# Six column tiles at once behind a norm, and weight splits placed by due time, in a two-layer decoder trunk

## The chip, the cores and the metric

One core of one Trainium2 chip runs the kernel. The metric is the device time of one execution in microseconds (us), lower is better; the number given is the median of three runs.

## What is computed

A two-layer decoder trunk on a sequence of 256 tokens, width 2048, in float32. Each layer projects x with w_in into the inputs of two parallel head groups (a gated linear recurrence and a sparse attention with compressed, selected and sliding branches), joins them with w_out, normalizes, runs a gated FFN with a causal convolution of width 3, and normalizes again:

```python
for l in range(DEPTH):                      # DEPTH = 2
    h = x @ w_in[l]                         # 2048 -> 6704 columns
    hq, hf, hi, hg, nq_, kc, vc, ks_, vs_, kw, vw, gt = jnp.split(h, offsets, axis=-1)
    o_h = hgrn2_mixer(hq, hf, hi, hg, lower_bounds[l], hgrn_norm_w[l])
    o_n = nsa_mixer(nq_, kc, vc, ks_, vs_, kw, vw, gt, pos, cmp_pe_k[l], cmp_pe_v[l],
                    cmp_w1_k[l], cmp_w2_k[l], cmp_w1_v[l], cmp_w2_v[l])
    y = jnp.concatenate([o_h, o_n], axis=-1) @ w_out[l]
    x = layer_norm(DN_ALPHA * x + y, ln1_g[l], ln1_b[l])
    f = conv_ffn(x, w_up[l], conv_w[l], conv_b[l], w_down[l])   # 2048 -> 2 x 5632 -> 2048
    x = layer_norm(DN_ALPHA * x + f, ln2_g[l], ln2_b[l])
```

## The kernel before, in words

**Numbers in two parts.** Every float32 operand is held as a high part (rounded to the format that TensorE takes in one pass) and a low part. `split` (L231 to L236) makes them from a raw tile: the high part `whi` with a copy on ScalarE (L235), or on GpSimd (L233) for some units, the low part `wlo` with a subtraction on VectorE (L236). x lies in SBUF with the features on the partitions, as `self.x[:, k, part, token]`, k = 0 to 15 being the contraction tile. One weight block of 128 x 128 costs two matmuls: L317 multiplies the high part with both parts of x (512 columns), L318 the low part with x's high part (256 columns).

**Units.** Weights come in units of 8 blocks, 512 KB, one DMA each, in the order in which they are used. `blocks` writes that order down as (column tile c, contraction tile k): mostly all 16 k of a column tile, then the next tile. Behind a norm, where x comes one k at a time, the first `OUTER = 4` column tiles are done together, k outermost, and then one tile after the other. `run` walks through all units of both layers: it issues loads 7 units ahead, splits 3 units ahead and then emits the unit's matmuls. There are 5 raw buffers and 4 pairs of split ones. A split is emitted at high priority; after a norm, `self.barriers` holds instructions of the norm behind which the next splits have to stand on VectorE. The order within each engine is set by a list scheduler that plans with these priorities; on the chip each engine runs its list in order.

**PSUM.** Accumulators are banks: three `pj`, two `ps_s`, two `ps_t`, one `ps_h`. Column tiles take `pj`; the fourth of the tiles done together takes `ps_h` (`wide`). When a tile's last k is done, `total` evicts it: a copy on ScalarE (L356), an addition on VectorE (L357).

**The norm** (`norm`) works feature tile by feature tile: `less` subtracts the mean for four at a time (L895), L950 scales, ScalarE makes the high part (L954; for k=0 VectorE does, L952), L957 the low part. Statistics come from matmuls with a matrix of ones; a few matmuls of constants (L865) stand in the wait. `dg` (L912, L917) spreads the scale over the partitions.

**The projection's order** is `u` in `layer`: column pairs 0 to 2 (compressed, selected and sliding keys, tiles 0 to 5, twelve units), then eight value-and-gate units (w_vg, 560 wide, L345 to L347), between which stand four units of the compressed branch (w_c1, L1113, not split, so that each keeps its raw buffer until it is used), then pair 3, the same again, and the rest. L1113 multiplies `F0`, which `cmp_in` (L429) makes on VectorE from column pair 0 after the rotation (L382, L384, L385); L414 makes the low part of a rotated key. GpSimd splits from the projection's unit 20 on.

**The start** (`head`) loads and splits the first four units in pieces, x's first quarter first.

Of the kernel before, what the change touches and what calls it, by code (L numbers as in the profile page):

```python
# [29 lines left out]
F32 = mybir.dt.float32  # L30
# [9 lines left out]
S = 256  # L40
D = 2048
KT = D // 128
DFF = 5632
FT = DFF // 128
# [21 lines left out]
VG = 280  # L66


def blocks(cts, nk, outer=0, head=0):

    first, rest = cts[:outer], cts[outer:]
    if head:
        o = [(c, k) for c in first for k in range(head)]
        o += [(c, k) for c in first for k in range(head, nk)]
    else:
        o = [(c, k) for k in range(nk) for c in first]
    return o + [(c, k) for c in rest for k in range(nk)]


N_IN = 40
OUTER = 4
ORDER_IN = blocks(range(6), KT, outer=OUTER) + blocks(range(6, N_IN), KT)
ORDER_OUT = blocks(range(KT), KT, outer=3, head=12)
ORDER_UP = blocks(range(2 * FT), KT, outer=OUTER)
ORDER_DOWN = blocks(range(KT), FT)


# [4 lines left out]
URGENT = 4  # L94
POOL = 20

WARM = 9, 7

ROW = (slice(0, 64), slice(64, 128))
# [2 lines left out]
class Trunk:  # L102
# [144 lines left out]

    def head(self, units):

        pieces = [(0, 0, 256), (1, 0, 384), (0, 256, 512), (1, 384, 768), (0, 512, 1024),  # L250
                  (1, 768, 1024), (2, 0, 512), (3, 0, 512), (2, 512, 1024), (3, 512, 1024)]
        raws = [self.t(self.wp, [128, 1024], F32, "raw", bufs=RAW_BUFS) for _ in units]
        outs = {n: [self.t(self.wp, [128, 1024], F32R, tag, bufs=PART_BUFS) for tag in ("whi", "wlo")]
                for n in (1, 3)}
        for i, lo, hi in pieces:
            self.nc.sync.dma_start(raws[i][:, lo:hi], units[i][0][:, lo:hi])
        for i, lo, hi in pieces:
            q = slice(lo, hi)
            if i in outs:
                self.split(outs[i][0][:, q], outs[i][1][:, q], raws[i][:, q])  # L260
            else:
                k = slice(2 * i + lo // 256, 2 * i + hi // 256)
                self.split(self.x[:, k, 0], self.x[:, k, 1],
                           raws[i][:, q].rearrange("p (k t) -> p k t", t=256))
        for n in outs:
            units[n][3](*outs[n])
# [28 lines left out]
            self.load = loads.get(i + 1)  # L295
            units[i][3](*parts.pop(i))

    def units(self, src, order, act, nk, done, pump=1, pre=None, last=None, wide=None):


        st = {}
        mm = self.nc.tensor.matmul

        def cb(hi, lo, n):
            for i, (c, k) in enumerate(order[n:n + 8]):
                if pre is not None and (c, k) in pre:
                    pre[c, k]()
                if c not in st:
                    st[c] = (self.t(self.ps_h, [128, 2, S], F32, "h") if c == wide
                             else self.t(self.pj, [128, 2, S], F32, "pj"))  # L310
                x, out, o = act(k), st[c], slice(128 * i, 128 * i + 128)
                if c == last:
                    for p in range(2):
                        mm(out[:, 0], hi[:, o], x[:, p], start=k == 0 and p == 0, stop=False,  # L314
                           skip_group_check=True)
                else:
                    mm(out, hi[:, o], x, start=k == 0, stop=False, skip_group_check=True)  # L317
                mm(out[:, 0], lo[:, o], x[:, 0], start=False, stop=k == nk - 1,  # L318
                   skip_group_check=True)
                if k == nk - 1:  # L320
                    done(c, st.pop(c))
                if pump == 2 and i == 3:
                    self.pump(1)
            self.pump(1)

        return [(src(n // 8), 1024, True, lambda hi, lo, n=n: cb(hi, lo, n), LOOK_SPLIT)
                for n in range(0, len(order), 8)]
# [543 lines left out]
    def norm(self, l, which, last):  # L871

        nc, v, act = self.nc, self.nc.vector, self.nc.scalar.activation
# [65 lines left out]
        else:  # L939
# [20 lines left out]
                    los.append(queue(lo_of()))  # L960
            los.append(queue(lo_of()))

            self.barriers.extend(los[5::2])
        urgent.close()


# [53 lines left out]
    def layer(self, l):  # L1020
# [134 lines left out]
        for hp in range(4):  # L1155
            dones += [d_h(hp, slot) for slot in (0, 2, 3)]
        tiles = self.units(lambda n: a["w_in"][l, n], ORDER_IN, xin, KT,
                           lambda c, ps: dones[c // 2](c, ps), pump=2, pre={(0, 0): pre_in},
                           wide=OUTER - 1)

        def pairs(p, n=1):
            return tiles[4 * p:4 * (p + n)]
# [12 lines left out]
        for step in PLAN.split():  # L1175
# [7 lines left out]
            else:  # L1183
# [3 lines left out]
        u += self.units(lambda n: a["w_out"][l, n], ORDER_OUT, lambda k: self.o[k // 2][:, k % 2], KT, self.d_res(l, 0),  # L1187
                        pre={(0, 0): pre_att, (0, 8): pre_hgr, (0, 12): pre_out}, last=KT - 1)
        u += self.units(lambda n: a["w_up"][l, n], ORDER_UP, xin, KT, self.d_ff(l),
                        pre={(0, 0): pre_up}, wide=OUTER - 1)  # L1190
        u += self.units(lambda n: a["w_down"][l, n], ORDER_DOWN, lambda k: self.f[:, k], FT,
                        self.d_res(l, 1), pre={(0, 0): pre_down}, last=KT - 1)
        return u
# [1 line left out]
    def build(self):  # L1195
        self.setup()
        units = []
        for l in range(L):
            units += self.layer(l)

        xs = [(self.a["x"][kq], 1024, False, lambda raw, kq=kq: self.in_x(kq, raw), LOOK_SPLIT)
              for kq in range(4)]
        consts = (None, 0, False, lambda raw: self.load_consts(), LOOK_SPLIT)
        x0, x1, x2, x3 = xs
        self.run([x0] + units[:1] + [x1] + units[1:3] + [x2] + units[3:4] + [x3] + [consts]
                 + units[4:])
        self.finish()


# [113 lines left out]
```

## Time and profile before

| what | us |
|---|---|
| three timed runs | 2548.55, 2549.75, 2551.13 |
| median | 2549.75 |
| the profiled execution, its own time | 2539.28 |
| its span, first to last instruction | 2537.5 |
| PE busy in it | 2476.0 (98%) |
| VectorE (DVE) busy | 1782.0 (70%) |
| ScalarE (ACT) busy | 1197.6 (47%) |
| GpSimd (POOL) busy | 428.4 (17%) |
| DMA engines, mean rate | 172 GB/s |

The profile is one execution, and its times count from its first instruction. PE is the matmul unit, PEld its weight loads, DVE VectorE, ACT ScalarE, POOL GpSimd, SP the queue that issues the loads. Matmuls overlap each other, so that one row's duration is longer than the distance to the next one's start, and a busy PE is not a PE at its peak. A row's "idle before" is the time in which its engine did nothing, with the instruction that ended it.

### The profile page before, as it was taken

Reading aid. Unit: us, or ns where it says so; the run is one execution under the profiler, and the core shown is the slowest. Engines: PE = TensorE matmul, PEld = TensorE weight load, DVE = VectorE, ACT = ScalarE, POOL = GpSimd, SP = SyncE. Lnnn points to the kernel's source line nnn. Section 1 sums busy time; section 2 is a strip of 40 time slices with the busy share of each in tenths; the row PEclk is TensorE's granted clock in tenths of the full one; section 3 lists DMA queues with packets and bytes.
Section 4 is the critical chain, followed back from the end, with each engine's and each line's share of the span. In section 5 each row is a group of like instructions: output and inputs, shape, how many; then the busy total and the mean of one; then the engine's idle time right before and its main releaser. Section 6 shows DMA issues by size and latency. Waiting matters only on the chain. (4 is left out here: it accounts for less than half of the span.)

```text
span 2537.5 us, 41283 instructions
## 1 busy us (share of the span) xinstructions
PE 2476.0 (98%) x15993; PEld 2123.9 (84%) x15993; DVE 1782.0 (70%) x2705; ACT 1197.6 (47%) x2189; POOL 428.4 (17%) x403
## 2 busy tenths in 40 slices
PE   8999999999999999999989999999999999999997
PEld 7888878878888888888878888788788888888887
DVE  8767876787777777555597678767877777774554
ACT  4144425455555555334341444354655555553343
POOL 0444551300000000001014445413000000000111
PEclk9999999999999999999999999999999999999999
DMA  7644344545556565656546444445556566656563
GB/s 244 211 159 132 127 142 133 175 155 186 186 188 184 190 184 188 186 190 190 166 152 210 153 133 130 136 141 158 174 187 188 190 190 186 189 185 189 178 198 105
DMA packets 122884, 436.99 MB, mean 172 GB/s; under 512 B 13760, under 2 KB 14528, under 8 KB 122688
## 3 DMA queue, kind: packets, MB, share of 16 engines
q1 hardware_dynamic: 122688, 434.35, 53.6%
q8 instruction: 126, 2.06, 0.3%
q14 instruction: 70, 0.57, 0.1%
HBM read 432.20 MB, written 2.10 MB: 171 GB/s over the span
## 5 line engine op out<-in xcount | busy, mean ns | idle before, releaser
L317 PE MATMUL pj<-x,whi 128*128 128x512 f32 x4032 | 1435.1, 398 | 18.6 <-ACT whi L235 6.3
L236 DVE TENSOR_TENSOR wlo<-raw,whi 128x1024 fp32r<-128x1024 f32 (+2 forms) x819 | 1015.8, 1242 | 584.4 <-ACT whi L235 499.7
L318 PE MATMUL pj<-x,wlo 128*128 128x256 f32 x4032 | 1138.3, 283 | 4.0 <-DVE wlo L236 3.8
L235 ACT ACTIVATE whi<-raw 128x1024 fp32r<-128x1024 f32 (+2 forms) x631 | 661.7, 1049 | 827.7 <-PE pj L317 647.7
L317 PEld LDWEIGHTS pj<-x,whi 128*128 128x128 f32 x4032 | 758.9, 188 | 202.5 <-DVE x L957 12.5
L318 PEld LDWEIGHTS pj<-x,wlo 128*128 128x128 f32 x4032 | 757.0, 188 | 9.2 <-DVE wlo L236 6.1
L317 PE MATMUL pj<-f,whi 128*128 128x512 f32 x1320 | 460.4, 393 | 0.0
L318 PE MATMUL pj<-f,wlo 128*128 128x256 f32 x1408 | 395.3, 281 | 0.0
L317 PEld LDWEIGHTS pj<-f,whi 128*128 128x128 f32 x1320 | 247.2, 187 | 56.3
L233 POOL TENSOR_SCALAR whi<-raw 128x1024 fp32r<-128x1024 f32 (+1 forms) x188 | 215.3, 1148 | 331.6 <-PE pj L347 148.9
L318 PEld LDWEIGHTS pj<-f,wlo 128*128 128x128 f32 x1408 | 266.3, 189 | 0.1
L810 POOL TENSOR_TENSOR s<-z 128x512 f32<-128x512 f32 x4 | 8.2, 2059 | 1208.9 <-DVE z L807 1208.9
L982 DVE SCALAR_TENSOR_TENSOR ct<-ch,par,ct 128x255 f32<-128x255 f32 (+1 forms) x352 | 168.2, 481 | 6.0
L317 PE MATMUL pj<-o,whi 128*128 128x512 f32 x480 | 167.1, 392 | 2.0 <-DVE o L582 1.9
L318 PE MATMUL pj<-o,wlo 128*128 128x256 f32 x512 | 143.3, 281 | 0.0
L317 PEld LDWEIGHTS pj<-o,whi 128*128 128x128 f32 x480 | 89.7, 187 | 22.5 <-DVE o L582 2.4
L980 ACT ACTIVATE ct<-ch,par 128x256 f32<-128x256 f32 x176 | 102.9, 587 | 3.0 <-DVE ch L357 3.0
L318 PEld LDWEIGHTS pj<-o,wlo 128*128 128x128 f32 x512 | 96.8, 189 | 0.4
L347 PE MATMUL pj<-whi,x 128*128 128x280 f32 (+1 forms) x256 | 90.6, 355 | 0.0
L346 PE MATMUL pj<-wlo,x 128*128 128x280 f32 (+1 forms) x256 | 89.8, 352 | 0.0
L345 PE MATMUL pj<-whi,x 128*128 128x280 f32 (+1 forms) x256 | 89.3, 353 | 0.0
L357 DVE TENSOR_TENSOR ch<-pj,ch 128x256 f32<-128x256 f32 x174 | 72.4, 418 | 0.0
(240 smaller groups left out, 2141.3 us busy)
## 6 DMA issues: line engine op xcount, KB each, us to landing
raw<-w_up SPq DMA_DIRECT2D x352, 512.0 KB, 3.5
raw<-w_down SPq DMA_DIRECT2D x176, 512.0 KB, 3.6
raw<-w_in SPq DMA_DIRECT2D x158, 512.0 KB, 3.8
raw<-w_out SPq DMA_DIRECT2D x64, 512.0 KB, 3.6
raw<-w_v SPq DMA_DIRECT2D x32, 512.0 KB, 3.8
raw<-w_vg SPq DMA_DIRECT2D x32, 280.0 KB, 3.6
raw<-w_c SPq DMA_DIRECT2D x16, 512.0 KB, 3.7
out<-z SPq DMA_DIRECT2D x3, 512.0 KB, 2.6
```

Of the source, the lines that this page charges most:

```text
L233: self.nc.gpsimd.tensor_scalar(hi, raw, 1.0, 0.0, op0=ALU.mult, op1=ALU.add)
L235: self.nc.scalar.activation(hi, raw, AF.Copy)
L236: return self.nc.vector.tensor_sub(lo, raw, hi.bitcast(F32))
L317: mm(out, hi[:, o], x, start=k == 0, stop=False, skip_group_check=True)
L318: mm(out[:, 0], lo[:, o], x[:, 0], start=False, stop=k == nk - 1, skip_group_check=True)
L345: mm(st[tt], xh, wh, start=first, stop=False, skip_group_check=True)
L346: mm(st[tt], xh, wl, start=False, stop=False, skip_group_check=True)
L347: mm(st[tt], xl, wh, start=False, stop=kt == KT - 1, skip_group_check=True)
L357: self.nc.vector.tensor_add(out, ps[:, 0], out)
L810: add(self.s1, self.z[:, 0:2], zz)
L980: act(t[:, c], h[:, c], AF.Identity, scale=w[2], bias=w[3])
L982: v.scalar_tensor_tensor(t[:, c, s:], h[:, c, :S - s], w[n], t[:, c, s:], op0=ALU.mult, op1=ALU.add)
```

## The change

- `OUTER` is 6: behind each norm, and at the start, six column tiles are done together, for k = 0 to 13; `TAIL = 2`: the last two k's are done column by column. The same holds for w_in and w_up. The weights' layout in memory follows the new order.
- The fourth of the six tiles takes `ps_h`, the fifth and sixth take the two `ps_t` banks.
- The splits that follow a norm stand behind the low parts number 3, 5, 6, 8, 9, 10, 12, 13 and 14 (`AFTER`, nine splits); before, behind every second one from 5 on (six splits).
- At the start the first four units are x's first quarter, two weight units and x's second quarter, and the other quarters and the constants are spread out accordingly.

```diff
-def blocks(cts, nk, outer=0, head=0):
+def blocks(cts, nk, outer=0, head=0, tail=0):
...
-        o = [(c, k) for k in range(nk) for c in first]
+        o = [(c, k) for k in range(nk - tail) for c in first]
+        o += [(c, k) for c in first for k in range(nk - tail, nk)]
     return o + [(c, k) for c in rest for k in range(nk)]
...
-OUTER = 4
-ORDER_IN = blocks(range(6), KT, outer=OUTER) + blocks(range(6, N_IN), KT)
+OUTER, TAIL = 6, 2
+ORDER_IN = blocks(range(N_IN), KT, outer=OUTER, tail=TAIL)
 ORDER_OUT = blocks(range(KT), KT, outer=3, head=12)
-ORDER_UP = blocks(range(2 * FT), KT, outer=OUTER)
+ORDER_UP = blocks(range(2 * FT), KT, outer=OUTER, tail=TAIL)
...
+AFTER = 3, 5, 6, 8, 9, 10, 12, 13, 14
...
-        pieces = [(0, 0, 256), (1, 0, 384), (0, 256, 512), (1, 384, 768), (0, 512, 1024),
-                  (1, 768, 1024), (2, 0, 512), (3, 0, 512), (2, 512, 1024), (3, 512, 1024)]
+        pieces = [(0, 0, 256), (1, 0, 384), (1, 384, 768), (0, 256, 512), (1, 768, 1024), (2, 0, 512),
+                  (0, 512, 1024), (2, 512, 1024), (3, 0, 512), (3, 512, 1024)]
...
-                    st[c] = (self.t(self.ps_h, [128, 2, S], F32, "h") if c == wide
-                             else self.t(self.pj, [128, 2, S], F32, "pj"))
+                    if 3 <= c < wide:
+                        st[c] = (self.t(self.ps_h, [128, 2, S], F32, "h") if c == 3
+                                 else self.t(self.ps_t, [128, 2, S], F32, "t"))
+                    else:
+                        st[c] = self.t(self.pj, [128, 2, S], F32, "pj")
...
-            self.barriers.extend(los[5::2])
+            self.barriers.extend(los[k] for k in AFTER)
...
-        self.run([x0] + units[:1] + [x1] + units[1:3] + [x2] + units[3:4] + [x3] + [consts]
-                 + units[4:])
+        self.run([x0] + units[:2] + [x1] + units[2:6] + [x2] + units[6:8] + [x3] + [consts]
+                 + units[8:])
```

The lines of the changed kernel stand six lower from the norm on (L957 is L963, L357 is L363, L1113 is L1119), two lower for L236 (L238).

**Place 1: VectorE, layer 0, the end of the norm ahead of w_up.** L957 or L963 writes the low part of x, L236 or L238 splits a unit of weights, L357 or L363 evicts a column tile (`ch`), 16 k's being done. Before:

```order
L236 TENSOR_TENSOR wlo_5543<-raw_5441,whi_5542 128x1024
L950 SCALAR_TENSOR_TENSOR z_4618<-z_4618,par_266,s_5377 128x256
L957 SCALAR_TENSOR_TENSOR x_73<-z_4618,par_266,x_73 128x256 x2
L236 TENSOR_TENSOR wlo_5565<-raw_5474,whi_5564 128x1024
L236 TENSOR_TENSOR wlo_5587<-raw_5496,whi_5586 128x1024
L236 TENSOR_TENSOR wlo_5609<-raw_5518,whi_5608 128x1024
L357 TENSOR_TENSOR ch_5622<-pj_5454,ch_5622 128x256
L357 TENSOR_TENSOR ch_5622<-pj_5457,ch_5622 128x256
```

And in the changed kernel, the same place:

```order
L238 TENSOR_TENSOR wlo_5611<-raw_5520,whi_5610 128x1024
L956 SCALAR_TENSOR_TENSOR z_4618<-z_4618,par_356,s_5377 128x256
L963 SCALAR_TENSOR_TENSOR x_73<-z_4618,par_356,x_73 128x256
L238 TENSOR_TENSOR wlo_5633<-raw_5542,whi_5632 128x1024
L238 TENSOR_TENSOR wlo_5655<-raw_5564,whi_5654 128x1024
L963 SCALAR_TENSOR_TENSOR x_73<-z_4618,par_356,x_73 128x256
L238 TENSOR_TENSOR wlo_5677<-raw_5586,whi_5676 128x1024
L363 TENSOR_TENSOR ch_5692<-pj_5454,ch_5692 128x256
L238 TENSOR_TENSOR wlo_5716<-raw_5608,whi_5715 128x1024
L363 TENSOR_TENSOR ch_5692<-pj_5457,ch_5692 128x256
```

Three splits stood together between the last low part and the evictions; now one stands there, and one more between two evictions.

**Place 2: TensorE, layer 1's projection, around the compressed branch.** L345 to L347 (L351 to L353) are value units, numbered by their `whi`; L1113 (L1119) takes one raw compressed unit with `sg`, the tile of F0. Before, in the middle of the fourth value unit (12728):

```order
L347 MATMUL pj_12712<-whi_12708,x_73 128x280
L345 MATMUL pj_12712<-whi_12728,x_73 128x280
L1113 MATMUL h_12746<-raw_12536,sg_12565 60x256 x4
L1113 MATMUL h_12746<-raw_12648,sg_12565 60x256 x4
L346 MATMUL pj_12712<-wlo_12729,x_73 128x280
```

Now, behind the seventh value unit (12795) and in the eighth (12813), followed by pair 3 (L323, L324):

```order
L351 MATMUL pj_12712<-whi_12813,x_73 128x280
L351 MATMUL pj_12713<-whi_12813,x_73 128x280
L1119 MATMUL h_12746<-raw_12538,sg_12637 60x256 x4
L1119 MATMUL h_12746<-raw_12604,sg_12637 60x256 x4
L1119 MATMUL h_12746<-raw_12726,sg_12637 60x256 x4
L1119 MATMUL h_12746<-raw_12769,sg_12637 60x256 x4
L352 MATMUL pj_12712<-wlo_12814,x_73 128x280
```

```order
L323 MATMUL pj_12907<-x_73,whi_12837 128x512
L323 MATMUL pj_12955<-x_73,whi_12878 128x512
L324 MATMUL pj_12907<-x_73,wlo_12838 128x256
```

The first compressed unit has moved behind three more value units, and all four stand together. Pair 3's second matmul takes the high half of its third unit (12878, from raw_12811).

**Place 3: VectorE, layer 1's projection, the way to F0 and on to pair 3.** Now (L388, L390, L391 are the rotation, L435 is `cmp_in`, L420 the keys' low part):

```order
L390 TENSOR_TENSOR rope_1952_12652<-rope_1952_12652,cf_76_360 128x512
L391 TENSOR_TENSOR hz_12622<-hz_12622 128x512
L391 TENSOR_TENSOR rope_1952_12652<-rope_1952_12652,rope_1953_12661 128x512
L435 TENSOR_TENSOR sg_12637<-hz_12622,par_12354 64x16x15 x3
L238 TENSOR_TENSOR wlo_12796<-raw_12744,whi_12795 128x560
L435 TENSOR_TENSOR sg_12637<-hz_12622,par_12354 64x16x15 x5
L420 TENSOR_TENSOR kl_12371<-rope_1952_12652,kh_12370 64x2x2x128 x2
L238 TENSOR_TENSOR wlo_12814<-raw_12751,whi_12813 128x560
```

Before, the split of the fourth value unit followed F0; now those of the fourth to the seventh (12729, 12754, 12772, 12796) stand ahead of its end. raw_12787, pair 3's first load, lies in the buffer of raw_12538, the first compressed unit; raw_12793 in that of raw_12751, the eighth value unit; raw_12811 in that of raw_12604, the second compressed unit.

## Rows read from the trace of the kernel before

**Rows 1.** The page: busy us (share of the span) and instructions of each engine

```profile
PE 2476.0 (98%) x15993; PEld 2123.9 (84%) x15993; DVE 1782.0 (70%) x2705; ACT 1197.6 (47%) x2189; POOL 428.4 (17%) x403
```

**Rows 2.** Stretches: length, busy us (instructions) PE, PEld, DVE, ACT, POOL; PEclk, DMA share, GB/s

```profile
509.20:537.80 28.60, 24.94 (x128) 19.58 (x128) 25.25 (x43) 16.30 (x27) 0.00 (x0) 1.00 0.34 107
537.80:548.90 11.10, 11.08 (x63) 9.66 (x64) 10.61 (x21) 8.65 (x14) 0.00 (x0) 1.00 0.69 237
1266.50:1295.30 28.80, 24.95 (x129) 19.59 (x129) 25.44 (x45) 16.24 (x27) 1.96 (x5) 1.00 0.34 110
```

**Rows 3.** Waits of PE: who for whom, us in total, times, longest

```profile
PE pj L317 <- DVE x L957: 5.1, 18, 0.4
...
PE pj L317 <- DVE hz L357: 2.2, 1, 2.2
```

**Rows 4.** Timeline, DVE behind layer 0's first norm: start, us, instruction [idle before]

```profile
516.85 1.22 DVE L895 TENSOR_TENSOR z<-z,c 128x1024 f32<-128x1024 f32 x1
518.11 0.48 DVE L950 SCALAR_TENSOR_TENSOR z<-z,par,s 128x256 f32<-128x256 f32 x1
518.51 0.48 DVE L957 SCALAR_TENSOR_TENSOR x<-z,par,x 128x256 fp32r<-128x256 f32 x1
518.90 1.22 DVE L236 TENSOR_TENSOR wlo<-raw,whi 128x1024 fp32r<-128x1024 f32 x1
...
533.94 3.49 DVE L236 TENSOR_TENSOR wlo<-raw,whi 128x1024 fp32r<-128x1024 f32 x3
537.35 1.08 DVE L357 TENSOR_TENSOR ch<-pj,ch 128x256 f32<-128x256 f32 x3
```

**Rows 5.** Timeline, PE, the fifth column tile's first matmul in that stretch

```profile
537.82 0.50 PE L317 MATMUL pj<-x,whi 128*128 128x512 f32 x1 [2.08 <-DVE ch L357]
```

**Rows 6.** Timeline, DVE, layer 1's projection from tile 0's rotation on

```profile
1297.38 2.77 DVE L382 TENSOR_TENSOR hz<-hz,cf 32x512 f32<-32x512 f32 x4
...
1302.99 0.74 DVE L236 TENSOR_TENSOR wlo<-raw,whi 128x560 fp32r<-128x560 f32 x1
1303.65 0.68 DVE L384 TENSOR_TENSOR hz<-hz,cf 128x512 f32<-128x512 f32 x1
...
1307.37 4.61 DVE L429 TENSOR_TENSOR sg<-hz,par 64x240 f32<-64x240 f32 x8
...
1312.67 2.78 DVE L414 TENSOR_TENSOR kl<-rope,kh 64x512 fp32r<-64x512 f32 x4
...
1326.47 5.03 DVE L414 TENSOR_TENSOR kl<-rope,kh 64x512 fp32r<-64x512 f32 x4
```

**Rows 7.** Timeline, POOL, the same projection

```profile
1326.77 1.30 POOL L233 TENSOR_SCALAR whi<-raw 128x1024 fp32r<-128x1024 f32 x1 [1.47 <-DMA raw<-w_in]
1328.32 3.70 POOL L233 TENSOR_SCALAR whi<-raw 128x1024 fp32r<-128x1024 f32 x3 [0.26 <-DMA raw<-w_in]
```

**Rows 8.** Timeline, PE, the same projection: first compressed matmul, last of pair 3

```profile
1312.08 0.43 PE L1113 MATMUL h<-raw,sg 128*60 128x256 f32 x2 [1.44 <-issue]
...
1341.68 0.28 PE L318 MATMUL pj<-x,wlo 128*128 128x256 f32 x1
```

**Rows 9.** Stretches of it: half clock behind the eviction wait; value units

```profile
1295.10:1298.50 3.40, 3.22 (x10) 2.74 (x11) 3.35 (x7) 0.00 (x0) 0.00 (x0) 0.50 0.84 261
1322.54:1327.94 5.40, 5.40 (x44) 5.40 (x43) 4.43 (x6) 3.09 (x6) 2.31 (x2) 1.00 0.92 310
```

**Rows 10.** The page, DMA issues: count, KB each, us to landing

```profile
raw<-w_in SPq DMA_DIRECT2D x158, 512.0 KB, 3.8
```

**Rows 11.** Timeline, DVE and PE, layer 0's projection

```profile
31.57 0.78 DVE L357 TENSOR_TENSOR hz<-pj,hz 128x256 f32<-128x256 f32 x2
...
10.69 0.51 PE L317 MATMUL pj<-x,whi 128*128 128x512 f32 x1 [1.03 <-ACT whi L235]
...
48.37 0.43 PE L1113 MATMUL h<-raw,sg 128*60 128x256 f32 x2 [2.30 <-issue]
...
78.79 0.28 PE L318 MATMUL pj<-x,wlo 128*128 128x256 f32 x1
```

More of the change, by code (lines that the diff above doesn't have):

```diff
@@ L248, in head @@
     def head(self, units):
-        pieces = [(0, 0, 256), (1, 0, 384), (0, 256, 512), (1, 384, 768), (0, 512, 1024),
-                  (1, 768, 1024), (2, 0, 512), (3, 0, 512), (2, 512, 1024), (3, 512, 1024)]
+        pieces = [(0, 0, 256), (1, 0, 384), (1, 384, 768), (0, 256, 512), (1, 768, 1024), (2, 0, 512),
+                  (0, 512, 1024), (2, 512, 1024), (3, 0, 512), (3, 512, 1024)]
         raws = [self.t(self.wp, [128, 1024], F32, "raw", bufs=RAW_BUFS) for _ in units]
         outs = {n: [self.t(self.wp, [128, 1024], F32R, tag, bufs=PART_BUFS) for tag in ("whi", "wlo")]
-                for n in (1, 3)}
+                for n in (1, 2)}
         for i, lo, hi in pieces:
@@ L261, in head @@
             else:
-                k = slice(2 * i + lo // 256, 2 * i + hi // 256)
+                k = slice(4 * (i > 0) + lo // 256, 4 * (i > 0) + hi // 256)
                 self.split(self.x[:, k, 0], self.x[:, k, 1],
@@ L296, in run, with units @@
             units[i][3](*parts.pop(i))
-    def units(self, src, order, act, nk, done, pump=1, pre=None, last=None, wide=None):
+    def units(self, src, order, act, nk, done, pump=1, pre=None, last=None, wide=0):
         st = {}
@@ L1158, in layer @@
                            lambda c, ps: dones[c // 2](c, ps), pump=2, pre={(0, 0): pre_in},
-                           wide=OUTER - 1)
+                           wide=OUTER)
         def pairs(p, n=1):
@@ L1189, in layer @@
         u += self.units(lambda n: a["w_up"][l, n], ORDER_UP, xin, KT, self.d_ff(l),
-                        pre={(0, 0): pre_up}, wide=OUTER - 1)
+                        pre={(0, 0): pre_up}, wide=OUTER)
         u += self.units(lambda n: a["w_down"][l, n], ORDER_DOWN, lambda k: self.f[:, k], FT,
```

## Prediction, made blind

> **What bounds the kernel now.** I read the page first: TensorE (PE) is busy for 98% of the span and VectorE (DVE) for 70% [rows 1]. Matmuls overlap, so this share hides lost time; I therefore count matmuls per stretch. A "pair" below is one 128x128 weight block against x: its high half over 512 columns and its low half over 256. After a norm's stretch 63 matmuls stand in 11.10 us [rows 2], so a pair takes 11.10 / 31.5 = 0.352 us at PE's pace. Second I read PE's waits: 18 short ones on x (5.1 us) and one of 2.2 us on an eviction, hz [rows 3]. Third, the stretches: behind the norm ahead of w_up in layer 0, 64 pairs take 28.60 us, the one ahead of layer 1's projection 28.80 us [rows 2]; the third norm that is followed by matmuls repeats the first, and the fourth ends the program. At pace 64 pairs are 22.5 us, so **each of these three norms costs PE about 6.1 us**.
>
> Fourth, DVE in such a stretch says why. Per contraction tile k it does L950 and L957, 0.40 + 0.39 us apart; a quarter of L895, 1.26 / 4 = 0.3; and it splits the weights that PE eats, L236, 1.22 us per unit of 8 pairs [rows 4]. With four column tiles a k feeds four pairs: DVE needs 0.8 + 0.3 + 0.6 = 1.7 us per k, PE 1.41. DVE is the bound, PE waits at each k. At the end all four tiles finish together, three splits stand ahead of the evictions in DVE's queue (533.94, then L357 at 537.35), and the fifth tile has no PSUM buffer until the first is evicted: 2.08 us [rows 4, 5].
>
> **The change part by part.** *Six tiles a k.* PE needs 6 x 0.352 = 2.11 us per k, DVE 0.8 + 0.3 + 6/8 x 1.22 = 2.0. Three units are split ahead, so over the group DVE has 16 x 1.1 + 10 x 1.22 = 29.8 us of work against PE's 96 x 0.352 = 33.8. The barrier list puts the nine splits behind low halves 3 to 14, each before the unit is due: unit 3 stands behind some four k's and is ready 4 x 1.1 + 1.2 = 5.6 us after the first matmul, due at 24 x 0.352 = 8.4; the last low half, k=15, stands behind the split of unit 12, whose buffers come free with unit 8 at 72 x 0.352 = 25.3, so it is ready near 25.3 + 1.2 (copy, taken like the split) + 1.2 + 0.4 = 28.1, due at 29.9. I take the x waits as gone.
>
> *Last two k's by column.* The first tile is finished five columns, 10 pairs = 3.5 us, before the group ends; its eviction costs a copy and an add (L357, 1.08 / 3 = 0.36 us [rows 4]) and may have one split in front. The seventh tile finds its buffer free, so the 2.08 us go too. The fourth to sixth tile take PSUM banks (h, t) that the norm's last matmuls have left by then. Gain at each of the two norms ahead of w_up: 6.1, less 0.1 for leftovers, **6.0 us, 12.0 for both**. Bounds: 2 (the eviction alone, if x stays the bound) and 6.1. DMA is idle for two thirds of these stretches [rows 2], so the earlier loads collide with nothing.
>
> *The projection of layer 1.* The same six microseconds are won up to the group's end, but what follows hangs on DVE, not on PE: the compressed branch needs F0 (L429), made on DVE from tiles 0 and 1, and these now finish later. In layer 1 the first matmul stands at 1266.5 [rows 2]; tile 0 is ready 86 x 0.352 = 30.3 later, DVE starts on it at 1297.3 (copy and semaphores 0.45, an estimate from the 0.4 of such rows). Then in its queue, as the order shows, until F0: 4 totals 1.4; 8 rotations 2 x 2.77; four of L384 and L385 at 0.65; 8 of L429 4.61; 5 value-weight splits at 0.70 (0.74 less the overlap of 0.04) [rows 6]. Sum 17.7, plus 0.3 for a wait on a high half, 18.0. GpSimd splits two value units (L233) in that time. Where it split 1024-wide units, four L414 took 5.03 us instead of 2.78 beside 5.0 us of GpSimd work [rows 6, 7], so DVE lost 0.45 us per microsecond; two units of about 1 us (an estimate: the wider ones take 3.70 / 3 = 1.23) cost 0.9. So F0 is done at D = 1297.3 + 18.9 = 1316.2; before, PE got it at 1312.08 [rows 8]. PE has by then run seven value units (a unit of 12 matmuls is 12 x 5.40 / 44 = 1.5 us [rows 9]), which the change moved ahead of the compressed units, and stands idle for some 5 us.
>
> The rest hangs on the raw ring. Three of its five buffers hold compressed weights until F0 comes, and column pair 3's first load needs the first of them. So: D + 0.3, load 3.8 [rows 10], landed D + 4.1. The second load waits for the low half of value unit 7, two L420 and a split behind F0, D + 2.1, and lands at D + 5.9; the third 1.55 later, as the GpSimd rows that wait for loads stand apart [rows 7], D + 7.4. PE takes that third unit's high half as its second matmul of the pair, so it starts at D + 7.4 + 1.2 = D + 8.6. The 32 pairs are 11.3 us. PE has then idled about 4 us: after an idle of 2.2 us the granted clock stood at 0.50 for 3.4 us [rows 9] (the 1.2 GHz level), worth 1.7 us. End: D + 8.6 + 11.3 + 1.7 = D + 21.6 = 1337.8; before, the same last matmul started at 1341.68 and ended 0.28 later [rows 8]. **Gain 4.2 us.** Bounds: -3 (each of the last two waits 3.5 us longer) and 12 (F0 early enough, no idle; the excess of this stretch over pace).
>
> *The start.* Old DVE took tile 0 at 31.57; the new tile 0 needs 25 pairs more, 8.8 us, less 4 pairs that now run before the wait at 10.69 (k=0 and 1 feed 12 instead of 8), 1.4: 39.0 [rows 11]. The same chain (17.4, as its first splits are done, + 0.9) gives D = 57.3 against 48.37 before, and the end of pair 3 at 57.3 + 21.6 = 78.9; before its last matmul ended at 79.07 [rows 11]. **Gain 0.2 us**; bounds -5 and 5. Loading two weight units ahead of x1 costs nothing I can see: x1 is needed only behind three units.
>
> *Sum:* 12.0 + 4.2 + 0.2 = **16.4 us**. The profiled execution took 2539.28 (span 2537.5 and 1.8 around it) and would take 2522.9; the median of the timed runs lies 10.5 higher, and I carry the difference over: 2549.75 - 16.4 = 2533.35, so **2533**.
>
> A rule to weigh: beside GpSimd's splits DVE loses about half of GpSimd's time [rows 6, 7]. The Trainium skill, "SBUF — State Buffer", section "Who interferes with whom", says that a DVE instruction with two SBUF inputs contends with a GpSimd instruction that reads SBUF, and describes the lock as exclusive: the loser blocks in full. By that, D would be later by 1.9 instead of 0.9 in both layers, and the time 2535; the row gives 2533, and I keep the row.
>
> **Rivals.** *The projections lose nothing behind the group* (12%): if DVE's chain hides and PE starts pair 3 without the idle, layer 1 gives 12 and the start 5, 29 in all: 2521. For it: before, DVE had short idles; against it: F0 and the ring are a fixed sequence.
>
> *They give back what the norms win* (20%): D later by 3 to 5 us in both layers (a load queue that waits in order, a clock that stays low), gain 4 to 11: 2539 to 2546.
>
> *It does not do what it says* (4%): DVE needs 2.0 of PE's 2.11 us per k; were its steps 10% longer, x would stay the bound, and only the evictions' 2 us per norm would go: gain 6 less what the projections cost, 2546 to 2550.
>
> *Slower* (4%): F0's chain runs beside GpSimd throughout. The place is the stretch from tile 0 to F0, the price the ratio 5.03 / 2.78 = 1.8 on 18 us, 14 us in each layer; with 16.4 won, 28 lost is 2561. It decides from 11 us a layer on (16.4 + 5.1 = 21.5). Against it: GpSimd has only two units to split there.
>
> **How the numbers follow.** The forecast, 60%: 2526 to 2539 (the two norms hold, the projections give -6 to +7 beside the sum). The range takes in most of the give-back and of the first rival's near side: **2522 to 2543**. A measurement here can tell about 0.2%, 5.1 us. Faster by more than that: 60 + 12 + 15 of the 20 + 3 of the 4 = 90%; within it: 5 + 1 = 6%; slower: 4%.
>
> **What would show it.** Right: behind both norms ahead of w_up 96 pairs run without a gap over 0.5 us, the wait on ch is gone, the low half of x 15 is ready 1 to 2 us before its matmul; in both layers PE idles ahead of the first compressed matmul for longer than before, near 1316 less what was won earlier, and again ahead of pair 3, with a stretch at half clock. Wrong: waits on x that remain (then the count per k failed), an F0 earlier than 1313 or later than 1319 (then the chain), or a stretch in the attention part that lengthens by microseconds, to which I gave nothing since its splits and their places are unchanged.

## The result and the profile after

| what | before | changed |
|---|---|---|
| median of five runs each, us | 2548.55 (2541.45 to 2551.13) | 2533.1 (2528.58 to 2534.88) |
| the profiled execution: own time, span | 2539.28, 2537.5 | 2533.10, 2531.3 |

The ratio is 0.9938, 95% interval 0.9918 to 0.9958: 15 us won, 2533.1 where 2533 was forecast (16.4 us, reckoned from 2549.75). The total came out as forecast; its parts did not. The changed kernel's page has nearly the same busy times as [rows 1]:

```profile
PE 2475.1 (98%) x15993; PEld 2129.5 (84%) x15993; DVE 1780.9 (70%) x2705; ACT 1195.5 (47%) x2189; POOL 432.8 (17%) x403
```

PE's waits in the whole program (who for whom, us in total, times, longest), to be held against [rows 3]:

```profile
PE pj L352 <- DVE wlo L238: 5.6, 5, 1.8
...
PE pj L323 <- POOL whi L235: 4.4, 2, 3.1
...
PE pj L323 <- DVE x L963: 1.0, 3, 0.3
```

18 waits on x of 5.1 us have become 3 of 1.0 us (the first matmul of each norm), and those on ch and hz are gone. New or longer are waits on splits, all in the projections. The stretches behind layer 0's first norm and ahead of layer 1's projection (columns as in [rows 2]):

```profile
514.30:536.90 22.60, 22.58 (x129) 19.71 (x130) 21.21 (x35) 13.10 (x20) 0.00 (x0) 1.00 0.46 141
536.90:548.05 11.15, 11.15 (x66) 9.76 (x65) 7.60 (x12) 5.52 (x9) 0.00 (x0) 1.00 0.74 233
1262.00:1284.60 22.60, 22.58 (x129) 19.75 (x130) 21.19 (x35) 13.08 (x20) 0.00 (x0) 1.00 0.40 119
```

64 pairs took 28.60 and 28.80 us in [rows 2]; now 22.60, which is the pace. On PE in layer 1's projection (start, duration, the idle before and who ended it) stands what the six microseconds turned into:

```profile
1304.19 0.40 PE L352 MATMUL pj<-wlo,x 128*128 128x280 f32 x1 [1.82 <-DVE wlo L238]
1310.34 0.40 PE L352 MATMUL pj<-wlo,x 128*128 128x280 f32 x1 [1.27 <-DVE wlo L238]
1313.29 3.67 PE L1119 MATMUL h<-raw,sg 128*60 128x256 f32 x32 [1.14 <-issue]
1319.73 0.49 PE L323 MATMUL pj<-x,whi 128*128 128x512 f32 x1 [1.29 <-POOL whi L235]
1323.31 0.79 PE L323 MATMUL pj<-x,whi 128*128 128x512 f32 x1 [3.08 <-POOL whi L235]
```

For all comparisons below I cut each trace at the first matmul of each norm that reads `dg`, which gives four stages: layer 0's projection and attention (in 0), its FFN (up 0), and the same for layer 1; 13.8 us remain at the end. A *mark* is the time from that matmul to the end of the n-th pair, counted by the low-half matmuls: 0.12 us behind the start of the n-th, where the next pair can start (its row ends 0.16 us later). "Runs" is the number behind the median; the ratios are to runs of the kernel before on the same chip.

| kernel | median (runs) | ratio, 95% interval | in 0 | up 0 | in 1 | up 1 |
|---|---|---|---|---|---|---|
| before | 2548.55 (5) | | 506.95 | 757.32 | 505.64 | 753.76 |
| before again | 2553.51 (1) | | 510.19 | 758.77 | 507.64 | 761.26 |
| changed | 2533.1 (5) | 0.9938 | 512.04 | 747.70 | 506.67 | 751.07 |
| changed again | 2533.46 (6) | 0.9942 [0.9924, 0.996] | 509.67 | 747.70 | 508.59 | 747.69 |
| w_up only | 2532.08 (6) | 0.9941 [0.9921, 0.9961] | 511.52 | 747.70 | 507.04 | 751.06 |
| projection only | 2552.48 (12) | 1.002 [1.0008, 1.0033] | 510.62 | 759.72 | 509.52 | 753.78 |
| w_up, no tail | 2534.14 (1) | | 508.68 | 751.19 | 507.45 | 751.20 |
| w_up, old split places | 2533.88 (1) | | 506.30 | 751.41 | 509.16 | 751.41 |
| w_up, four tiles with tail | 2551.28 (1) | | 511.02 | 758.84 | 507.04 | 758.76 |
| compressed units late | 2533.77 (5) | 0.9947 [0.9933, 0.996] | 511.06 | 747.69 | 509.18 | 751.05 |
| GpSimd later | 2523.58 (4) | 0.9905 [0.9888, 0.9921] | 506.22 | 747.70 | 502.66 | 747.70 |
| keys late | 2527.84 (4) | 0.9917 [0.9902, 0.9932] | 510.69 | 747.70 | 506.20 | 747.70 |
| both of these | 2518.74 (4) | 0.9891 [0.9867, 0.9915] | 502.98 | 751.06 | 500.78 | 747.70 |
| foreign matmuls | 2539.06 (1) | | 512.54 | 752.42 | 508.68 | 749.80 |

### The profile page after: what moved, and what is told of

It is laid out like the page before. It is cut to its first block, busy times and chain, and to the rows that moved or that the text cites. A ratio compares the mean times of both kernels' runs of the same rounds, so it can differ in the third digit from the quotient of the medians.

```text
span 2531.3 us, 41286 instructions
## 1 busy us (share of the span) xinstructions
PE 2475.1 (98%) x15993; PEld 2129.5 (84%) x15993; DVE 1780.9 (70%) x2705; ACT 1195.5 (47%) x2189; POOL 432.8 (17%) x403
## 4 chain that ended last, share of the span: by engine, by line
PE 87%; DVE 8%; issue 2%; POOL 1%; DMA 1%; ACT 1%; SPq 0%; ACTq 0%; POOLq 0%; DVEq 0%
PE pj L323 49%; PE pj L324 26%; DVE wlo L238 2%; PE pj L320 1%; PE t L323 1%; PE pj L353 1%; PE pj L352 1%; PE pj L351 1%; DVE rope L388 1%; PE h L645 1%; DMA raw<-w_in 1%; POOL whi L235 1%; PE s L580 1%; DVE sg L435 1%; PE h L323 1%
## 5 line engine op out<-in xcount | busy, mean ns | idle before, releaser
L238 DVE TENSOR_TENSOR wlo<-raw,whi 128x1024 fp32r<-128x1024 f32 (+2 forms) x819 | 1016.0, 1242 | 580.4 <-ACT whi L237 496.4
L323 PE MATMUL pj<-x,whi 128*128 128x512 f32 x3904 | 1387.2, 397 | 10.5 <-ACT whi L237 5.1
L324 PE MATMUL pj<-x,wlo 128*128 128x256 f32 x3904 | 1101.7, 283 | 0.6 <-DVE wlo L238 0.5
L323 PEld LDWEIGHTS pj<-x,whi 128*128 128x128 f32 x3904 | 735.4, 189 | 180.2 <-ACT whi L237 5.1
L324 PEld LDWEIGHTS pj<-x,wlo 128*128 128x128 f32 x3904 | 733.5, 188 | 6.2 <-DVE wlo L238 2.1
L323 PE MATMUL pj<-f,whi 128*128 128x512 f32 x1320 | 460.4, 393 | 0.0
L324 PE MATMUL pj<-f,wlo 128*128 128x256 f32 x1408 | 395.3, 281 | 0.0
L323 PEld LDWEIGHTS pj<-f,whi 128*128 128x128 f32 x1320 | 247.2, 187 | 56.3
L324 PEld LDWEIGHTS pj<-f,wlo 128*128 128x128 f32 x1408 | 266.3, 189 | 0.1
L323 PE MATMUL pj<-o,whi 128*128 128x512 f32 x480 | 168.0, 394 | 2.0 <-DVE o L588 1.9
L324 PE MATMUL pj<-o,wlo 128*128 128x256 f32 x512 | 143.4, 281 | 0.0
L323 PEld LDWEIGHTS pj<-o,whi 128*128 128x128 f32 x480 | 89.8, 187 | 23.2 <-DVE o L588 2.4
L324 PEld LDWEIGHTS pj<-o,wlo 128*128 128x128 f32 x512 | 96.8, 189 | 0.4
L351 PE MATMUL pj<-whi,x 128*128 128x280 f32 (+1 forms) x256 | 89.7, 357 | 1.8 <-POOL whi L235 1.8
L353 PE MATMUL pj<-whi,x 128*128 128x280 f32 (+1 forms) x256 | 91.1, 358 | 0.0
L363 DVE TENSOR_TENSOR ch<-pj,ch 128x256 f32<-128x256 f32 x170 | 70.9, 418 | 4.0 <-ACT ch L362 4.0
```

What stands on the lines that cost most here:

```text
L238: return self.nc.vector.tensor_sub(lo, raw, hi.bitcast(F32))
L351: mm(st[tt], xh, wh, start=first, stop=False, skip_group_check=True)
L353: mm(st[tt], xl, wh, start=False, stop=kt == KT - 1, skip_group_check=True)
L363: self.nc.vector.tensor_add(out, ps[:, 0], out)
```

## The experiments

**Each kernel once more.** The two profiled executions differ by 6.2 us, the medians by 15. Both kernels ran again, unedited.

> The kernel before, unchanged, for a second trace of it. In the first trace a pair of matmuls took 0.3529 us all through layer 0's w_up and 0.3489 us all through layer 1's. Theory A (the pace of a stretch is drawn anew in each execution): other values in these two stretches, and a span that differs by 3 us or more from 2537.5. Theory B (the pace belongs to the program): the same values in the same stretches, and a span within 1 us.

> The changed kernel, unchanged, for a second trace and more times. In the first trace a pair took 0.3489 us in layer 0's w_up and 0.3529 in layer 1's, the reverse of the kernel before. Theory A (drawn anew in each execution): other values. Theory B (belongs to the program): the same ones. In both, the 96 pairs behind each of the norms ahead of w_up end 36.0 us after the statistics' spread, and pair 3 of layer 1 at 77.5; the ratio to the kernel before is 0.990 to 0.997.

The stage times differ from execution to execution: the same program gave 753.76 and 761.26 for up 1. Two things make the difference. In the first execution of before, the eviction waits ahead of w_up left the clock alone; in the second the granted clock fell behind both of them. Stretches of before, run again, columns as in [rows 2]:

```profile
541.90:545.30 3.40, 3.40 (x12) 2.90 (x11) 3.40 (x8) 1.27 (x3) 0.00 (x0) 0.51 0.81 288
1808.20:1811.60 3.40, 3.40 (x13) 2.92 (x12) 3.40 (x8) 1.84 (x4) 0.00 (x0) 0.50 0.91 322
```

That is the 1.2 GHz level, and the mark of 96 pairs stood at 43.74 instead of 42.28. The other is the pace of the matmul pairs (last section): up 1 ran at 0.3489 us a pair in the first execution and at 0.3533 in the second.

**The two halves of the change.** In one kernel w_up alone keeps the new order, in the other the projection and the start do:

```diff
-ORDER_IN = blocks(range(N_IN), KT, outer=OUTER, tail=TAIL)
+ORDER_IN = blocks(range(6), KT, outer=4) + blocks(range(6, N_IN), KT)
```

```diff
-ORDER_UP = blocks(range(2 * FT), KT, outer=OUTER, tail=TAIL)
+ORDER_UP = blocks(range(2 * FT), KT, outer=4)
```

(with `wide`, the split places and the start to match).

> The new order and the new split places for w_up alone; the projection and the start as before. My theory (the norms ahead of w_up pay 6.2 us each, the projections give back 5 in layer 0 and 1 in layer 1): 12 us faster than before, ratio 0.995, and 5 to 6 us faster than the whole change by stretches of the trace. Rival (the projections pay as well, and the loss seen in layer 0 is the pace of its matmuls): 12 us faster than before and slower than the whole change by 2 to 4.

> The new order, start and split places for the projection alone; w_up as before. My theory: 5 to 6 us slower than before by stretches of the trace (layer 0 to its first norm near 512 us instead of 507, layer 1's 506.7 instead of 505.6), ratio 1.002. Rival (the projections pay): 2 to 4 us faster, ratio 0.999.

"Projection only" came as my theory had it. Of "w_up only" the ratio did (0.9941, 0.995 forecast), but it does not beat the whole change by 5 to 6 us in its stages: its two projection stages take 1018.6 us, those of the changed kernel 1018.7 and 1018.3. The whole gain is in w_up; the projection half by itself is slower, by 0.1 to 0.3%. In w_up 96 pairs end 36.02 us behind `dg` (42.28 and 42.08 before). In layer 1's projection 96 pairs end at 36.03 instead of 43.75, and then 128 pairs (pair 3 is the last 32) at 77.82 instead of 77.54: everything is given back by the end of pair 3.

**Which part of the change does it, in w_up.** Three kernels on top of "w_up only":

```diff
-OUTER, TAIL = 6, 2
+OUTER, TAIL = 6, 0
```

> The new order for w_up alone (projection and start as before), six column tiles with the contraction outermost to the end: the last two contraction tiles are not done column by column. If the tail is what takes the eviction wait away (my theory), the waits on x stay gone, 64 pairs stand at 24.8 us behind the norm's first matmul as with the tail, but ahead of the seventh tile PE waits about 2 us for its PSUM buffer in both layers, so that 96 pairs stand at 36.0 or less and the seventh tile starts near 38. The rival, that with three fewer splits ahead of the evictions the wait is gone without a tail: a gap of under 0.7 us there.

```diff
-            self.barriers.extend(los[5::2] if which else [los[k] for k in AFTER])
+            self.barriers.extend(los[5::2])
```

> The new order for w_up alone, with the splits behind every second low half from the sixth on, as before the change (six barriers instead of nine, the first behind the sixth). If the places of the splits matter (my theory): unit 3 is due 24 pairs = 8.4 us behind the first matmul, its split now stands behind the sixth low half, 6 x 1.1 + 1.2 = 7.8 us, still in time; the later units come one per 2.2 + 1.2 us on VectorE where PE eats one per 2.8 us, so the lag grows by 0.6 a unit and PE waits on wlo from the fifth unit on, some 2 to 3 us in all by the end of the norm: 96 pairs near 38 to 39 us instead of 36.0. The rival, that the order alone does it and the places don't matter: 36.0 to 36.5.

```diff
-OUTER, TAIL = 6, 2
+OUTER, TAIL = 4, 2
```

(the third with the old split places too).

> For w_up alone four column tiles as before and the old places of the splits, but the last two contraction tiles column by column. If six tiles are what takes the waits on x away (my theory), the waits on x stay, 4 us in each norm, and only the eviction wait of 2 us goes: 64 pairs stand near 26.5 us, 96 pairs near 40 us (42.2 before, 36.0 with the whole change). The rival, that the tail alone gives most of it: 96 pairs below 38.

My theory fell in all three; in the first two the rival came. Without the tail 96 pairs end at 36.01 and 128 at 47.46, against 36.03 and 47.34 at the same pace with it: the tail, as it was written down, is worth 0.1 us. The old split places cost 0.35 (96 pairs at 36.36). Four tiles with a tail win nothing: 64 pairs at 28.6, 96 at 43.7 and 43.8, since the eviction wait stayed whole and the clock fell behind it. On DVE and PE of that kernel:

```profile
538.01 3.49 DVE L238 TENSOR_TENSOR wlo<-raw,whi 128x1024 fp32r<-128x1024 f32 x3
541.41 1.08 DVE L363 TENSOR_TENSOR ch<-pj,ch 128x256 f32<-128x256 f32 x3
```

```profile
537.54 0.40 PE L323 MATMUL h<-x,whi 128*128 128x512 f32 x1
...
538.14 0.50 PE L323 MATMUL pj<-x,whi 128*128 128x512 f32 x1
...
538.60 0.39 PE L323 MATMUL pj<-x,whi 128*128 128x512 f32 x1
...
538.95 0.40 PE L323 MATMUL pj<-x,whi 128*128 128x512 f32 x1
...
539.31 0.40 PE L323 MATMUL h<-x,whi 128*128 128x512 f32 x1
...
541.88 0.52 PE L323 MATMUL pj<-x,whi 128*128 128x512 f32 x1 [2.06 <-DVE ch L363]
```

But these rows also show that the tail was not carried out there: column by column, two `h` would stand side by side at the end, and PE's order is that of the kernel before. So the third kernel says nothing of a tail that is carried out beside four tiles.

**Six tiles a k, with the new split places, give all but 0.1 us of the gain**, the eviction's part too: "no tail" shows it. With DVE ahead of PE one split instead of three stands in front of the evictions. Six tiles with neither the tail nor the new places were not run. In the changed kernel, too, the tail is not carried out behind the norms. Its PE, the end of the group in layer 0's w_up (84 pairs stand before it):

```profile
543.86 0.39 PE L323 MATMUL pj<-x,whi 128*128 128x512 f32 x1
544.09 0.28 PE L324 MATMUL pj<-x,wlo 128*128 128x256 f32 x1
544.21 0.39 PE L323 MATMUL pj<-x,whi 128*128 128x512 f32 x1
544.44 0.28 PE L324 MATMUL pj<-x,wlo 128*128 128x256 f32 x1
544.56 0.40 PE L323 MATMUL pj<-x,whi 128*128 128x512 f32 x1
544.79 0.40 PE L323 MATMUL h<-x,whi 128*128 128x512 f32 x1
545.02 0.63 PE L323 MATMUL t<-x,whi 128*128 128x512 f32 x2
...
545.96 0.39 PE L323 MATMUL pj<-x,whi 128*128 128x512 f32 x1
```

Three `pj`, `h` and two `t` come once for k=14 and then again for k=15: the list scheduler moved k=14 of all six columns ahead of the first k=15. I take the reason to be that it plans x 15 late, behind the splits: with the old split places, where the low half of x 15 was done at 531.27, 6.7 us ahead of the group's first k=14, the tail came out as written. In PE's rows there two `h` stand side by side:

```profile
540.54 0.40 PE L323 MATMUL h<-x,whi 128*128 128x512 f32 x1
...
540.90 0.39 PE L323 MATMUL h<-x,whi 128*128 128x512 f32 x1
```

In the changed kernel the first tile is complete after 91 pairs, not after 86, and its eviction on DVE follows at once:

```profile
546.93 0.42 DVE L363 TENSOR_TENSOR ch<-pj,ch 128x256 f32<-128x256 f32 x1 [2.02 <-ACT ch L362]
```

**Where the projection loses it: the ring of five raw buffers, or VectorE?** First the compressed units behind all eight value units (the first branch's also behind pair 3), so that they hold no raw buffers while F0 is made:

```diff
 u = pairs(0, 3)
 for br in range(2):
-    if br:
+    u += self.tok_units(lambda kq, br=br: a["w_vg"][l, br, kq], VG, 2, d_vg(br))
+    if not br:
         u += pairs(3)
...
+    u += cmp_units(br)
```

> The changed kernel with the four compressed units of each branch placed behind all eight value units of that branch (and so the first ones behind pair 3) instead of between them, so that they no longer hold raw buffers while F0 is made. If it is F0 and the raw ring that give back the six microseconds behind the group (my theory), pair 3 starts without the idle times of 1.1 to 3.1 us ahead of it, pair 3's end in layer 1 stands at 70 to 73 us plus the value units' part behind the norm instead of 77.5 less the compressed units' 2 us; over the stage some 4 to 7 us are won in each layer: 2520 to 2526, ratio to before 0.990. The rival, that VectorE is simply short of time there and PE waits for it at another place: within 2 us of the changed kernel, 2531 to 2535, ratio 0.994.

The rival. Pair 3 ended sooner, at 69.1 us, which is 77.5 less the compressed units' 3.7 and another 4.7; but PE lost it all behind pair 3, and 256 pairs stood at 178.65 (177.91 and 180.00 in the two executions of the changed kernel). A new wait of 4.18 us had come up, on a PSUM bank whose eviction stood in DVE's queue:

```profile
1337.33 0.54 PE L351 MATMUL pj<-whi,x 128*128 128x280 f32 x1 [4.18 <-DVE rope L363]
```

The loss moved with DVE's queue. So two kernels take work from DVE there. One gives the high halves of units 20 to 39 to ScalarE; GpSimd then stands idle beside DVE:

```diff
-POOL = 20
+POOL = 40
```

> The changed kernel in which GpSimd makes high halves only from the projection's unit 40 on instead of from unit 20, so that ScalarE, busy 10 of 41 us between 1301 and 1342, makes those of units 20 to 39 and nothing stands beside VectorE's work there. If VectorE is what bounds the projection behind its first six tiles (my theory; it is busy 39.3 of those 41 us, with a rotation at 4.26 us instead of 2.77 and a split at 1.95 instead of 1.22 beside GpSimd), the 12.2 us of GpSimd work at 0.45 us of VectorE's time each are 5.5 us: pair 3 ends 3 to 5 us sooner than the 77.5 us of the changed kernel in layer 1, and the time is 2523 to 2528. The rival, that the raw ring and its loads set the pace there whatever VectorE does: pair 3's end within 1 us of 77.5, 2531 to 2535.

The other puts off the rotation of column pairs 1 and 2:

```diff
         def d_vc(t):
             box["F1"] = self.cmp_in(l, 1, t)
+            for br in range(2):
+                self.k_in(box.pop(f"k{br}"), br)
...
         def d_k(br):
-            return lambda t: self.k_in(t, br)
+            return lambda t: box.__setitem__(f"k{br}", t)
```

(and gives pairs 1 and 3 parts of `hz` buffers to wait in).

> The changed kernel in which the rotations and low parts of the selected and the sliding keys (column pairs 1 and 2) are put off until the second branch's F1 is made, behind pair 3, where VectorE is busy only 20 of 33 us; pair 1 takes the free third of pair 0's buffer for that. If VectorE bounds the stretch (my theory), 4.1 us leave the way to F0 and some 14 us the stretch up to pair 3's end: pair 3 ends 5 to 9 us sooner in layer 1 (68 to 72 us instead of 77.5) and, with the work fitting into VectorE's 13 idle us behind, 160 pairs stand 3 to 7 us sooner: 2520 to 2527, ratio to before 0.990. The rival, that PE loses the time behind pair 3 instead, as with the compressed units placed late: 128 pairs sooner, 256 pairs within 1.5 us of the 177.9 of the changed kernel, 2531 to 2535.

Then the two together:

> The changed kernel with both: the keys' rotations put off behind pair 3, and no GpSimd work before the projection's unit 40. Each alone took VectorE work out of the stretch from 1301 to 1342 (39.3 us of 41 before, 32.9 and 32.1 with the one and the other) and gave 10 and 5 us. If it is VectorE's work that counts (my theory), the two add where they touch different work: pair 3 ends near 67 to 69 us in layer 1 (77.5, 73.9 and 70.9 in the other three), 160 pairs stand at 101 to 104 us, and the time is 2515 to 2521. The rival, that once one of them is in another resource (the raw ring, PE itself) is the bound: no better than the former alone, 2521 to 2526.

GpSimd later and both came as my theory had them: 9.9 and 14.7 us below "changed again" (which ran on another chip), and their projection stages are shorter by as much (1008.9 and 1003.8 us for the two together, 1018.3 in "changed again"). Keys late by itself is half a miss: pair 3 ended at 70.94 as I had it, but 160 pairs only 0.8 us and 256 pairs 0.8 us sooner than in the first execution of the changed kernel, as the rival had it. Its projection stages gained 1.4 us over "changed again", whose up stages in the profiled execution are the same; the rest of the 5.6 us between the two medians can't be laid to a stage, as the other runs have no trace. PE waited for F1 there, which DVE made among the rotations put off:

```profile
1341.23 4.12 PE L1127 MATMUL h<-raw,sg 128*60 128x256 f32 x24 [3.50 <-DVE sg L435]
```

The same stretch, 41 us from 41.3 us behind `dg` on, of the kernel before, the changed kernel, GpSimd later, keys late and both, one row each, columns as in [rows 2]:

```profile
1305.53:1346.53 41.00, 36.35 (x249) 31.65 (x248) 38.26 (x55) 12.33 (x25) 11.34 (x12) 1.00 0.59 193
```

```profile
1301.00:1342.00 41.00, 32.12 (x189) 27.49 (x188) 39.33 (x56) 9.97 (x21) 12.18 (x11) 0.88 0.51 159
```

```profile
1295.18:1336.18 41.00, 34.80 (x217) 29.87 (x215) 37.17 (x60) 18.90 (x33) 0.00 (x0) 0.92 0.57 181
```

```profile
1299.65:1340.65 41.00, 33.84 (x210) 28.02 (x210) 32.10 (x47) 6.80 (x15) 14.62 (x12) 0.92 0.53 171
```

```profile
1295.30:1336.30 41.00, 37.36 (x257) 31.35 (x258) 33.16 (x54) 16.97 (x29) 0.00 (x0) 1.00 0.60 201
```

In the changed kernel DVE is busy 39.33 of the 41 us, and it was 38.26 before the change. Without GpSimd beside it, it gets through 60 instructions instead of 56 in 37.17 us; without the rotations it has 8 to 9 us to spare. PE does 21 to 68 matmuls more. Pair 3 ends at 77.5, 73.85, 70.94 and 69.04 us, 160 pairs at 109.7, 105.5, 108.9 and 103.5.

The ring is close behind, though. In the changed kernel pair 3's second matmul (1323.31, above) waits for a high half that hangs on the ring, and the third for the first unit's low half, which DVE finished at 1324.33, so that by these rows freeing one of the two alone would have won 1 us at most:

```profile
1318.09 4.26 DVE L388 TENSOR_TENSOR rope<-rope,cf 32x512 f32<-32x512 f32 x4
1322.38 1.95 DVE L238 TENSOR_TENSOR wlo<-raw,whi 128x1024 fp32r<-128x1024 f32 x1
```

GpSimd later changed PE's order as well: that low half comes second there, and PE waits 1.85 us for it. In keys late DVE itself stands idle ahead of the same split, for a load and GpSimd's high half:

```profile
1316.00 1.23 DVE L238 TENSOR_TENSOR wlo<-raw,whi 128x1024 fp32r<-128x1024 f32 x1 [7.09 <-POOL whi L235]
```

So **VectorE's work holds the changed kernel's projection back in this stretch**, with the loads next, and VectorE again behind it as long as GpSimd stands beside it: only without GpSimd do the put-off keys pay in the stages, by another 5.1 us. Both together, 2518.74, beat the kernel before and the changed one: 0.9891 of the kernel before, where the changed one had 0.9942.

How much GpSimd costs DVE can be read from the same forms in two kernels between 1301 and 1342, changed (first two rows) and GpSimd later:

```profile
L388 DVE TENSOR_TENSOR rope<-rope,cf 32x512 f32<-32x512 f32 x8 | 7.0, 869 | 0.1
...
L238 DVE TENSOR_TENSOR wlo<-raw,whi 128x1024 fp32r<-128x1024 f32 x4 | 5.5, 1396 | 0.0
```

```profile
L238 DVE TENSOR_TENSOR wlo<-raw,whi 128x1024 fp32r<-128x1024 f32 x4 | 4.8, 1222 | 0.0
...
L388 DVE TENSOR_TENSOR rope<-rope,cf 32x512 f32<-32x512 f32 x4 | 2.7, 683 | 0.1
```

869 ns against 683 and 1396 against 1222: with the four other large forms (both L435, L420, the 560-wide L238) the excess sums to 3.8 us beside 12.18 us of GpSimd, 0.31 per microsecond where I had taken 0.45. (One short instruction on DVE, the gate's L1054, took 1009 ns against 227; with it the sum is 4.6 us, 0.38.) The Trainium skill, "SBUF — State Buffer", section "Who interferes with whom", says that a DVE instruction with two SBUF inputs contends with a GpSimd instruction that reads SBUF; the rows agree. By its exclusive lock, under which the loser blocks in full, I had put DVE's loss at 1.0 per microsecond, about three times this; the measurement decides.

## Why the prediction was right, point by point

**Six tiles a k: right.** 6.0 us per norm were forecast; 6.27 and 6.05 came (42.28 to 36.01, 42.08 to 36.03). But for the first matmul of each norm the waits on x are gone, and the low half of x 15 is done at 542.69. That is 3.3 us ahead of its first matmul, which stands at 545.96 because the tail was not carried out; with the tail it would have been some 1.5, an estimate from the place of pair 86 (1 to 2 forecast).

```profile
542.21 0.48 DVE L963 SCALAR_TENSOR_TENSOR x<-z,par,x 128x256 fp32r<-128x256 f32 x1
```

**Last two k's by column: the step failed.** "The first tile is finished five columns, 10 pairs, before the group ends" holds in layer 0's projection alone; behind the norms it is 5 pairs. The term came out because six tiles and the new split places removed the eviction wait by themselves, and I had given the tail what was theirs.

**Layer 1's projection: gain 4.2 forecast, next to nothing measured.** Pair 3 ends 77.50 and 77.04 us behind `dg` in the two executions (77.54 and 77.52 before); I had 73.5. By my own steps, in the first execution: tile 0, "ready 86 x 0.352 = 30.3 later", was ready after 91 pairs, and DVE took it at 1294.66, 34.9 behind `dg` instead of 33.0. The chain to F0 was sized well: first compressed matmul at 1313.29, 18.6 later (18.9 forecast), so 53.55 instead of 51.9, **1.65 us**. Pair 3 started at F0 + 10.0 instead of F0 + 8.6, **1.4**. The 32 pairs and the clock took 13.9 instead of 13.0, **0.9**; the granted clock stood at 0.50 for twice the time of [rows 9]:

```profile
1321.90:1328.70 6.80, 5.11 (x15) 4.03 (x16) 6.77 (x7) 0.00 (x0) 3.07 (x2) 0.50 0.45 131
```

Together 3.95 of the 4.0 missing. The first of the three is the tail's: five pairs more are 1.76 us. The second is the ring's: GpSimd began the third unit's high half, right behind its load, at 1322.07, F0 + 8.8, where I had the load landed at F0 + 7.4.

```profile
1322.07 3.16 POOL L235 TENSOR_SCALAR whi<-raw 128x1024 fp32r<-128x1024 f32 x2 [0.26 <-DMA raw<-w_in]
```

What I did not see is that DVE would have held PE there in any case: I had followed its queue to F0 and left it there, and the first low half of pair 3 came only at 1324.33, F0 + 11.0. The 5 us of idle time that I had put ahead of the first compressed matmul came at three places, 1.82, 1.27 and 1.14 us, the first two for splits in the same queue. And "to which I gave nothing" was wrong behind pair 3: 160 pairs stood at 109.7 and 111.9 (108.9 and 109.1 in the two executions of before).

**Layer 0's projection: right at its place.** There the tail was carried out; the first compressed matmul stood at 56.47 (57.3 forecast) and pair 3's last row ended at 78.42 (78.9). What followed I had not forecast either: 160 pairs at 113.68 and 112.71, where the two executions of before had 110.18 and 113.40.

**The sum came out by what I had not forecast.** Averaged over the four executions with the old order in w_up (before, before again, projection only, four tiles with tail), an up stage took 757.8 us; over four with the whole new one (changed, changed again, w_up only, compressed units late) 749.0. That is 8.8 a layer, 17.6 in all, where I had 12. Of the 8.8, 6.2 are the waits. The rest is two things: in four of the eight old up stages the clock fell behind the eviction wait, 1.5 us each, which no longer happens, and the pairs ran at the longer pace in six of the eight old stages but in three of the eight new ones (eight of eighteen, with the other kernels that do six tiles in w_up, "foreign matmuls" left out). The first belongs to the change; that the second does is not shown. The projections lost 0.9 and 1.4 us by the same averages (with the new order: changed, changed again, projection only; with the old: before, before again, w_up only, four tiles with tail), where I had +4.4. 17.6 - 2.3 = 15.3, the measured 15. That w_up gave 5.6 us more than forecast and the projections 6.7 less, so that the sum hit, is luck.

## What to carry to other kernels

Count the work of the engine that feeds as well as that of the one that waits: here VectorE was busy for 38.3 of 41 us already before the change, and PE's waits, once gone, came back at the next place. What helped was to take work from VectorE, by moving GpSimd's work from its side and putting off what nobody needs yet. An order that is written into a list need not be the order that a scheduler emits: read the emitted order at the very place on which a term rests. And when two profiled executions differ by less than the medians, cut several into stages before naming a cause.

## What was not expected of the hardware

Pairs of matmuls without any wait hold one pace for hundreds of pairs, and it is one of two: 0.3489 or 0.3533 us through all of w_up. It changes from execution to execution of one program and makes up most of the spread of an up stage (some 1300 pairs at 0.0044 us are 5.8 us; w_down, at 0.3533 or 0.3467 in its first part, often gives back 2.4 of them: 751.07 against 747.70). One kernel puts a foreign matmul ahead of every sixteenth column tile of w_up:

```diff
+                if nk == KT and len(order) == 2 * FT * KT and k == 0 and c in (16, 32, 48, 64):
+                    h = self.t(self.ps_h, [128, 512], F32, "h")
+                    mm(h[:, :S], self.ones, self.cf[:, 128:384], start=True, stop=True,
+                       skip_group_check=True)
```

> The changed kernel with one foreign matmul (ones by constants, 256 columns, into a bank that nothing reads) ahead of column tiles 16, 32, 48 and 64 of w_up in both layers, eight in all, about 0.4 us each; the output does not depend on them. If the pace of the matmul pairs, which in every run held one of 0.349 or 0.353 us through all of w_up, is fixed anew wherever another matmul stands between (my theory), the five pieces of w_up run at paces of their own, some at 0.349 and some at 0.353 or at another of the values seen (0.3467 to 0.3545). The rival, that the pace belongs to the program's position or to the execution as a whole: one pace in all five pieces.

The pieces of layer 0 ran at 0.3533, 0.3533, 0.3489, 0.3533 and 0.3489 us, those of layer 1 at 0.3489, 0.3489, 0.3533, 0.3489 and 0.3533: three of the four breaks flipped the pace in each layer, and the two layers mirror each other. Stretches of 80 us from the second to the fifth piece of layer 0, columns as in [rows 2]; the matmul counts follow the pace:

```profile
610.00:690.00 80.00, 80.00 (x455) 69.71 (x454) 56.47 (x84) 44.64 (x70) 0.00 (x0) 1.00 0.57 187
700.00:780.00 80.00, 80.00 (x460) 70.07 (x459) 57.45 (x85) 44.98 (x71) 0.00 (x0) 1.00 0.59 190
790.00:870.00 80.00, 80.00 (x455) 69.70 (x454) 56.47 (x84) 44.77 (x71) 0.00 (x0) 1.00 0.58 187
880.00:960.00 80.00, 80.00 (x461) 70.04 (x460) 57.36 (x85) 45.62 (x72) 0.00 (x0) 1.00 0.57 189
```

So in this one execution the pace was set at the breaks and did not belong to the execution as a whole. Why one break in four leaves it, and what sets it at the start, stays open.
